# Variance over rows on one core: the first load issued as eight strided loads, ahead of the critical section

## The chip, the cores and the metric

The kernel runs on one core of a Trainium2 chip. The metric is device time in microseconds, the median of several executions. An execution under the hardware profiler gives the trace that is read here: times in it count from the first instruction of the profiled execution, and its span ends with the last one.

## The reference

```python
batch, seq, dim = 32, 512, 1024
x = np.random.randn(batch, seq, dim).astype(np.float32)
mean_sq = np.mean(x**2, axis=-1)
sq_mean = np.mean(x, axis=-1)**2
return (mean_sq - sq_mean).astype(np.float32)
```

There are 16,384 rows of 1,024 float32 values, 67.1 MB. Each row gives one number, its variance. Every byte of x is read once, and the output is 64 KB.

## The kernel before

**Layout.** The 16,384 rows are spread over 128 partitions as 128 columns, so that a "column" is one row of x on each partition. `BLOCKS` (L42) maps columns to rows: columns 0 to 15 are the first 2,048 rows, with 16 consecutive rows (64 KB) on each partition; the other 112 columns follow in the same way, with 112 consecutive rows on each partition.

**Loads.** All loads and stores are issued by SyncE (SP), in program order. Columns 0 to 95 come in six loads of 16 columns (8.4 MB each, 64 KB per partition) into two buffers in turn, `xt[0]` and `xt[1]` (L146 to L149). The first two loads wait for nothing. Each later one waits until VectorE has counted up `done` for the group that used the buffer before (L148). The last 32 columns (the end) come in loads of 8, 8, 5, 4, 2, 2, 1 and 1 columns and two halves of one column, each with a semaphore of its own (L151 to L160). The loads' helper is `load` (L89), and its DMA instruction stands on L93. A load raises its semaphore by 16 when it has landed.

**Compute.** Of each group of 16 columns, ScalarE takes 6 (`NACT`) and VectorE 10. ScalarE makes a mean in one pass (L117) and the sum of squared deviations in a second (L122). VectorE takes statistics of the two halves of a column (L113) and joins them (L216). VectorE waits for `landed` in a loop of 3 turns (L203 to L217), tells ScalarE by `go`, and after the group counts `done`. The waits in the loops are made by `take` (L107), which waits and then subtracts; its instructions stand on L109. GpSimd copies the results of a turn (L165) and joins a part of the end columns.

**The end.** The columns of the end are split over ScalarE and VectorE by `END_WHO`. Three stores (L100) follow one another: columns 0 to 15, then to the end of the fourth end load, then the rest. SP issues the last store when ScalarE and VectorE have done their last columns (L302, L303).

**Order and sections.** Tiles and semaphores come from the tile framework's pools. The whole work stands in one critical section (L144), which the framework opens with a signal from GpSimd and closes with a drain on every engine that reports to GpSimd. Behind it the context is closed (L306 to L308): two all-engine barriers, between which GpSimd clears the framework's semaphores. Only then SP waits for the three stores (L309) and clears their semaphore (L310). In the profile, the start-up of the program (constants and an all-engine barrier) stands on L325, the section's own instructions on L144, the closing on L308.

Of the kernel before, what the change touches and what calls it, by code (L numbers as in the profile page):

```python
# [11 lines left out]
def kernel(  # L12
# [14 lines left out]
    nc = tc.nc  # L27
# [9 lines left out]
    ncols = N // P  # L37
# [18 lines left out]
    EARLY = 4  # L56
    HEAD = 128

    pool = ctx.enter_context(tc.tile_pool(name="pool", bufs=1))
    xt = [pool.tile([P, GROUP, D], FP32, name=f"xt{b}") for b in range(NBUF)]  # L60
    xt_end = pool.tile([P, ncols - END0 - FIRST, D], FP32, name="xt_end")
    mv = pool.tile([P, 2, ncols], FP32, name="mv")
    stage = pool.tile([P, PER_TURN, 2], FP32, name="stage")
    stats = pool.tile([P, PER_TURN, 2, 6], FP32, name="stats")
    stats_join = pool.tile([P, JOINED, 2, 6], FP32, name="stats_join")
    stats_end = pool.tile([P, ncols - END0, 4, 6], FP32, name="stats_end")
    neg_mean = pool.tile([P, PER_TURN], FP32, name="neg_mean")
    neg_mean_end = pool.tile([P, ncols - END0], FP32, name="neg_mean_end")
    two = pool.tile([P, JOINED, 2], FP32, name="two")
    mu = pool.tile([P, JOINED, 1], FP32, name="mu")  # L70
    dev = pool.tile([P, JOINED, 4], FP32, name="dev")
    psum = ctx.enter_context(tc.tile_pool(name="psum", bufs=1, space=bass.MemoryType.PSUM))
    junk = [pool.tile([P, D], mybir.dt.bfloat16, name=f"junk{i}") for i in range(ACT_BATCH)]
    junk_sq = [psum.tile([P, D], FP32, name=f"junk_sq{i}") for i in range(ACT_BATCH)]

    sync, act, dve, gps = nc.sync, nc.scalar, nc.vector, nc.gpsimd
    landed = [tc.alloc_semaphore(f"landed{b}") for b in range(NBUF)]
    NEND = len(END_LOADS) + len(PIECES)
    landed_end = [tc.alloc_semaphore(f"landed_end{b}") for b in range(NEND)]
    go = tc.alloc_semaphore("go")  # L80
    act_done = tc.alloc_semaphore("act_done")
    done = tc.alloc_semaphore("done")
    copied = tc.alloc_semaphore("copied")
    dve_step = tc.alloc_semaphore("dve_step")
    act_step = tc.alloc_semaphore("act_step")
    gps_step = tc.alloc_semaphore("gps_step")
    stored = nc.alloc_semaphore("stored")

    def load(dst, c0, n, sem, f0=0, f=D):  # L89
        b0, pitch, row0 = next(b for b in BLOCKS if b[0] <= c0 < b[0] + b[1])  # L90
        assert c0 + n <= b0 + pitch
        ap = [[pitch * D, P], [D, n], [1, f]] if n > 1 else [[pitch * D, P], [1, f]]
        sync.dma_start(  # L93
            out=dst,
            in_=dataclasses.replace(xf, offset=(row0 + c0 - b0) * D + f0, ap=ap),
        ).then_inc(sem, 16)
# [47 lines left out]
    with tc.tile_critical(sync_engine=ENG.Pool, no_gpsimd_drain=True):  # L144

        for g in range(TURNS * NBUF):  # L146
            if g >= NBUF:
                sync.wait_ge(done, g - NBUF + 1)  # L148
            load(xt[g % NBUF], g * GROUP, GROUP, landed[g % NBUF])  # L149
        sync.wait_ge(done, (TURNS - 1) * NBUF + 1)  # L150
        c = END0  # L151
        for b, n in enumerate(END_LOADS):
            k = c - END0
            buf, k = (xt[0], k) if k < FIRST else (xt_end, k - FIRST)
            load(buf[:, k : k + n, :] if n > 1 else buf[:, k, :], c, n, landed_end[b])
            c += n
        f = 0
        for b, n in enumerate(PIECES, len(END_LOADS)):
            load(end_col(c)[:, f : f + n], c, 1, landed_end[b], f, n)
            f += n  # L160

        gps.sem_inc(copied, 1)
        for t in range(TURNS):
            gps.wait_ge(done, (t + 1) * NBUF)
            gps.tensor_copy(  # L165
                out=mv[:, 1, t * PER_TURN : (t + 1) * PER_TURN], in_=stage[:, :, 1]
            ).then_inc(copied, 1)

        part = stats_join.rearrange("p n h (e s) -> p n (h e) s", s=3)
        mean, m2 = part[:, :, :, 1], part[:, :, :, 2]  # L170
        gps.wait_ge(dve_step, 1)
        steps = [
            lambda: gps.tensor_tensor(out=two, in0=mean[:, :, 0:2], in1=mean[:, :, 2:4], op=ALU.add),  # L173
            lambda: gps.tensor_tensor(out=mu, in0=two[:, :, 0:1], in1=two[:, :, 1:2], op=ALU.add),
            lambda: gps.tensor_scalar(out=mu, in0=mu, scalar1=0.25, scalar2=None, op0=ALU.mult),
            lambda: gps.tensor_tensor(out=dev, in0=mean, in1=mu.to_broadcast([P, JOINED, 4]), op=ALU.subtract),
            lambda: gps.tensor_tensor(out=dev, in0=dev, in1=dev, op=ALU.mult),
            lambda: gps.tensor_scalar(out=dev, in0=dev, scalar1=D / 4.0, scalar2=None, op0=ALU.mult),  # L178
            lambda: gps.tensor_tensor(out=dev, in0=dev, in1=m2, op=ALU.add),
            lambda: gps.tensor_tensor(out=two, in0=dev[:, :, 0:2], in1=dev[:, :, 2:4], op=ALU.add),  # L180
            lambda: gps.tensor_tensor(out=mu, in0=two[:, :, 0:1], in1=two[:, :, 1:2], op=ALU.add),
        ]
        k = 0
        runs = []
        for j, c in enumerate(joined):
            if runs and runs[-1][1] + runs[-1][2] == c:
                runs[-1][2] += 1
            else:
                runs.append([j, c, 1])
        for j, c, n in runs:  # L190
            steps.append(
                lambda j=j, c=c, n=n: gps.tensor_scalar(  # L192
                    out=mv[:, 1, c : c + n], in0=mu[:, j : j + n, 0],
                    scalar1=1.0 / D, scalar2=None, op0=ALU.mult,
                )
            )
        for k, step in enumerate(steps):
            if k:
                gps.wait_ge(gps_step, k)
            step().then_inc(gps_step, 1)  # L200
        gps_steps = len(steps)

        with nc.Fori(0, TURNS, engines=[ENG.DVE]):  # L203
            take(dve, copied, 1)
            for b in range(NBUF):
                take(dve, landed[b], 16)
                dve.sem_inc(go, 1)
                mine = range(b * GROUP + NACT, (b + 1) * GROUP)
                for j in mine:
                    last = halves(stats[:, j, :, :], xt[b][:, j - b * GROUP, :])  # L210
                last.then_inc(dve_step, 1)
                take(dve, dve_step, 1)
                for j in mine:
                    if j == mine[-1]:
                        take(dve, act_done, 1)
                    last = dve.bn_aggr(out=stage[:, j, :], in_=stats[:, j, :, :])  # L216
                last.then_inc(done, 1)  # L217
        n = 0
        waiting = None
        seen = -1  # L220
        for b, c, who in end_cols:
            if who != "D":
                continue
            if b != seen:
                dve.wait_ge(landed_end[b], 16)
                seen = b
            col = end_col(c)
            if c in joined:
                last = halves(stats_join[:, joined.index(c), :, :], col)
                if c == joined[-1]:  # L230
                    last.then_inc(dve_step, 1)
                    n += 1
                continue
            st = stats_end[:, c - END0, :2, :]
            dve.bn_stats(out=st[:, 0, :], in_=col[:, :H])  # L235
            if waiting:
                waiting()
            n += 1
            dve.bn_stats(out=st[:, 1, :], in_=col[:, H:]).then_inc(dve_step, 1)  # L239
            dve_step_of.setdefault(b, n)  # L240

            def waiting(n=n, c=c, st=st):
                dve.wait_ge(dve_step, n)
                return dve.bn_aggr(out=mv[:, :, c], in_=st)  # L244

        c = ncols - 1
        st = stats_end[:, c - END0, : len(PIECES), :]
        f = 0
        for i, size in enumerate(PIECES):
            dve.wait_ge(landed_end[len(END_LOADS) + i], 16)  # L250
            last = dve.bn_stats(out=st[:, i, :], in_=end_col(c)[:, f : f + size])  # L251
            if i == 0:
                waiting()
            f += size
        n += 1
        last.then_inc(dve_step, 1)
        dve.wait_ge(dve_step, n)
        dve.bn_aggr(out=mv[:, :, c], in_=st).then_inc(dve_step, 1)
        dve_steps = n + 1

        act.preload_act_table(ACTF.Square)  # L261
# [15 lines left out]
        for b in range(len(END_LOADS)):  # L277
            mine = [c for bb, c, who in end_cols if bb == b and who == "A"]
            if not mine:
                continue  # L280
# [60 lines left out]
```

## Time and profile before

| What | Value |
|---|---|
| Median of 3 executions | 163.78 us (163.43 to 163.83) |
| The profiled execution's own time | 163.64 us |
| Its span, first to last instruction | 161.9 us |
| VectorE busy | 103.7 us (64%) |
| ScalarE busy | 106.3 us (66%) |
| DMA packets of SP's queue, share of 16 engines | 96.7% |
| Mean rate over the span | 415 GB/s |
| First VectorE statistics start | 23.11 us |
| Second group's statistics start | 42.44 us |
| Last store issued | 160.06 us |

The profiled execution's time is 1.7 us longer than its span, and lies 0.14 us below the median. The DMA share is the mean over the core's 16 DMA engines of the time that their packets take. Packets of the six large loads are 64 KB each, one for each partition, so that each of the 16 engines carries 8 packets of a load.

### The profile page before, as it was taken

To read this page: it belongs to the slowest core of one execution; us is meant where nothing else is said; L and a number is where in the kernel's file an instruction comes from. 1 tells how busy PE (TensorE), PEld (TensorE's weight loads), DVE (VectorE), ACT (ScalarE), POOL (GpSimd) and SP (SyncE) were. 2 spreads that over 40 slices of the span, in tenths; PEclk is the share of its full clock that TensorE was granted. 3 is DMA by queue.
4 is the path that set the end of the run, shared out by engine and by line. 5 is a ranking of instruction groups with operands and counts; after the bars stand their busy time and mean duration, and the time that the engine had idled before them with its cause. 6 is when DMAs were issued, how large, how long until landed. Compare 5 with 4: busy or idle time off the path is not lost. (4 is left out here: it accounts for less than half of the span.)

```text
span 161.9 us, 579 instructions
## 1 busy us (share of the span) xinstructions
DVE 103.7 (64%) x232; ACT 106.3 (66%) x189; POOL 3.6 (2%) x18
## 2 busy tenths in 40 slices
DVE  0000029980599607994099921999039979999994
ACT  3000029990599807996099941999139999799985
POOL 0000000000000000000000000000000000005100
DMA  7969979989988998998997997997989999999991
GB/s 263 518 275 502 518 324 453 518 356 421 518 389 389 518 405 372 518 421 356 518 437 340 518 437 340 518 470 308 518 348 429 421 470 405 400 434 411 423 394 27
DMA packets 2738, 67.19 MB, mean 415 GB/s; under 512 B 688, under 2 KB 688, under 8 KB 1200
## 3 DMA queue, kind: packets, MB, share of 16 engines
q1 hardware_dynamic: 2736, 67.18, 96.7%
q14 instruction: 2, 0.02, 0.1%
HBM read 67.11 MB, written 0.07 MB: 415 GB/s over the span
## 5 line engine op out<-in xcount | busy, mean ns | idle before, releaser
L113 DVE BATCH_NORM_STATS2 stats<-xt 128x6 f32<-128x512 f32 x120 | 71.8, 678 | 49.9 <-DVEq L109 49.9
L117 ACT ACTIVATE junk<-xt 128x1024 bf16<-128x1024 f32 x41 | 42.7, 1042 | 50.4 <-ACTq L109 49.3
L122 ACT ACTIVATE junk_sq<-xt,neg_mean 128x1024 f32<-128x1024 f32 x36 | 39.7, 1104 | 1.5
L113 DVE BATCH_NORM_STATS2 stats_join<-xt 128x6 f32<-128x512 f32 x22 | 13.2, 677 | 0.0
L216 DVE BATCH_NORM_AGGREGATE stage<-stats 128x2 f32<-128x12 f32 x60 | 6.0, 166 | 6.2 <-DVEq L109 5.3
L117 ACT ACTIVATION_READ_ACCUMULATOR junk<-xt 128x1 f32 x41 | 7.6, 186 | 0.0
L122 ACT ACTIVATE junk_sq<-xt_end,neg_mean_end 128x1024 f32<-128x1024 f32 x6 | 6.7, 1111 | 0.1
L122 ACT ACTIVATION_READ_ACCUMULATOR junk_sq<-xt,neg_mean 128x1 f32 x36 | 6.7, 186 | 0.0
L117 ACT ACTIVATE junk<-xt_end 128x1024 bf16<-128x1024 f32 x6 | 6.3, 1046 | 0.4 <-DMA xt_end<-in_x_dram 0.2
L235 DVE BATCH_NORM_STATS2 stats_end<-xt_end 128x6 f32<-128x512 f32 x9 | 6.1, 675 | 0.0
L239 DVE BATCH_NORM_STATS2 stats_end<-xt_end 128x6 f32<-128x512 f32 x9 | 5.8, 642 | 0.0
L122 ACT ACTIVATE junk_sq<-xt,neg_mean_end 128x1024 f32<-128x1024 f32 x5 | 5.5, 1106 | 0.1
L165 POOL COPY mv<-stage 128x32 f32<-128x32 f32 x3 | 0.6, 210 | 133.0 <-DVE stage L216 133.0
L261 ACT ACT_TABLE_LOAD x1 | 1.3, 1283 | 1.3 <-PEq L325 1.3
L244 DVE BATCH_NORM_AGGREGATE mv<-stats_end 128x2 f32<-128x12 f32 x9 | 1.7, 191 | 0.0
L251 DVE BATCH_NORM_STATS2 stats_end<-xt_end 128x6 f32<-128x512 f32 x2 | 1.3, 668 | 0.1
L117 ACT ACTIVATION_READ_ACCUMULATOR junk<-xt_end 128x1 f32 x6 | 1.1, 188 | 0.0
L122 ACT ACTIVATION_READ_ACCUMULATOR junk_sq<-xt_end,neg_mean_end 128x1 f32 x6 | 1.1, 186 | 0.0
L122 ACT ACTIVATION_READ_ACCUMULATOR junk_sq<-xt,neg_mean_end 128x1 f32 x5 | 0.9, 188 | 0.0
L173 POOL TENSOR_TENSOR two<-stats_join 128x22 f32<-128x22 f32 x1 | 0.3, 252 | 12.9 <-DVE stats_join L113 12.9
L192 POOL TENSOR_SCALAR mv<-mu 128x6 f32<-128x6 f32 (+1 forms) x2 | 0.5, 236 | 0.2
L178 POOL TENSOR_SCALAR dev<-dev 128x44 f32<-128x44 f32 x1 | 0.3, 331 | 0.1
(12 smaller groups left out, 2.3 us busy)
## 6 DMA issues: line engine op xcount, KB each, us to landing
xt<-in_x_dram SPq DMA_DIRECT2D x2, 4096.0 KB, 19.5
xt_end<-in_x_dram SPq DMA_DIRECT2D x1, 2560.0 KB, 29.8
xt_end<-in_x_dram SPq DMA_DIRECT2D x1, 2048.0 KB, 34.2
xt_end<-in_x_dram SPq DMA_DIRECT2D x2, 1024.0 KB, 37.1
xt_end<-in_x_dram SPq DMA_DIRECT2D x2, 512.0 KB, 39.3
xt_end<-in_x_dram SPq DMA_DIRECT2D x2, 256.0 KB, 40.0
xt<-in_x_dram SPq DMA_DIRECT2D x6, 24.5
out_dram<-mv SPq DMA_DIRECT2D x1, 52.5 KB, 4.4
```

The lines of the kernel that those rows point to most:

```text
L113: last = dve.bn_stats(out=st[:, h, :], in_=xcol[:, h * H : (h + 1) * H])
L117: return act.activation(out=junk[i], in_=xcol, func=ACTF.Copy, scale=-S / D, accum_out=nm)
L122: return act.activation(out=junk_sq[i], in_=xcol, func=ACTF.Square, scale=S, bias=nm, accum_out=var)
L165: gps.tensor_copy(out=mv[:, 1, t * PER_TURN : (t + 1) * PER_TURN], in_=stage[:, :, 1]).then_inc(copied, 1)
L173: lambda: gps.tensor_tensor(out=two, in0=mean[:, :, 0:2], in1=mean[:, :, 2:4], op=ALU.add),
L192: lambda j=j, c=c, n=n: gps.tensor_scalar(out=mv[:, 1, c : c + n], in0=mu[:, j : j + n, 0], scalar1=1.0 / D, scalar2=None, op0=ALU.mult,)
L216: last = dve.bn_aggr(out=stage[:, j, :], in_=stats[:, j, :, :])
L235: dve.bn_stats(out=st[:, 0, :], in_=col[:, :H])
L239: dve.bn_stats(out=st[:, 1, :], in_=col[:, H:]).then_inc(dve_step, 1)
L244: return dve.bn_aggr(out=mv[:, :, c], in_=st)
L251: last = dve.bn_stats(out=st[:, i, :], in_=end_col(c)[:, f : f + size])
L261: act.preload_act_table(ACTF.Square)
```

## The change

It does three things. First, the load of group 0 becomes eight DMAs. DMA p0 carries partitions p0, p0+8, p0+16, ..., p0+120, that is 16 partitions, with all 16 columns (64 KB on each). All eight raise one new semaphore, `first`; SP waits until it is 128 and then raises `landed[0]` by 16. Second, these eight DMAs and the load of group 1 are issued ahead of any critical section, and the framework's context is closed and compiled directly behind them, so that its barriers and clearing come there. Third, the rest of the program stands behind the closed context: tiles are allocated directly and not from pools, the semaphores are the kernel's own, and SP clears them, after the last store is issued and before it waits for the stores. The code of the rest is the same, one level less indented.

```diff
+    STRIDE = 8
...
-    pool = ctx.enter_context(tc.tile_pool(name="pool", bufs=1))
-    xt = [pool.tile([P, GROUP, D], FP32, name=f"xt{b}") for b in range(NBUF)]
+    def sbuf(name, shape, dtype):
+        return nc.alloc_sbuf_tensor(name, shape, dtype).ap()
+    xt = [sbuf(f"xt{b}", [P, GROUP, D], FP32) for b in range(NBUF)]
...
-    landed = [tc.alloc_semaphore(f"landed{b}") for b in range(NBUF)]
+    landed = [nc.alloc_semaphore(f"landed{b}") for b in range(NBUF)]
...
+    first = nc.alloc_semaphore("first")
     stored = nc.alloc_semaphore("stored")
+    sems = [*landed, *landed_end, go, act_done, done, copied, dve_step, act_step, gps_step, first]
...
-    with tc.tile_critical(sync_engine=ENG.Pool, no_gpsimd_drain=True):
-
-        for g in range(TURNS * NBUF):
-            if g >= NBUF:
-                sync.wait_ge(done, g - NBUF + 1)
-            load(xt[g % NBUF], g * GROUP, GROUP, landed[g % NBUF])
...
+    for p0 in range(STRIDE):
+        dma = sync.dma_start(
+            out=xt[0][p0::STRIDE, :, :],
+            in_=dataclasses.replace(
+                xf, offset=p0 * SMALL * D, ap=[[STRIDE * SMALL * D, P // STRIDE], [D, GROUP], [1, D]]
+            ),
+        ).then_inc(first, 16)
+        tc.no_tile_sem_insts.add(dma.ins.name)
+    for g in range(1, NBUF):
+        dma = load(xt[g], g * GROUP, GROUP, landed[g])
+        tc.no_tile_sem_insts.add(dma.ins.name)
     ctx.close()
     tc.close()
     tc.compile()
+
+    sync.wait_ge(first, STRIDE * 16)
+    sync.sem_inc(landed[0], 16)
+
+    for g in range(NBUF, TURNS * NBUF):
+        sync.wait_ge(done, g - NBUF + 1)
+        load(xt[g % NBUF], g * GROUP, GROUP, landed[g % NBUF])
...
     store(early, ncols)
+    sync.sem_clear(range(sems[0].num, sems[-1].num + 1))
     sync.wait_ge(stored, 48)
     sync.sem_clear(stored)
```

More of the change, by code (lines that the diff above doesn't have):

```diff
@@ L56 @@
     EARLY = 4
+    STRIDE = 8
     HEAD = 128
-    pool = ctx.enter_context(tc.tile_pool(name="pool", bufs=1))
-    xt = [pool.tile([P, GROUP, D], FP32, name=f"xt{b}") for b in range(NBUF)]
[L61 to L73, printed above, removed]
@@ L74, with psum @@
-    junk_sq = [psum.tile([P, D], FP32, name=f"junk_sq{i}") for i in range(ACT_BATCH)]
+    def sbuf(name, shape, dtype):
+        return nc.alloc_sbuf_tensor(name, shape, dtype).ap()
+    def psum(name, shape, dtype):
+        return nc.alloc_psum_tensor(name, shape, dtype).ap()
+    xt = [sbuf(f"xt{b}", [P, GROUP, D], FP32) for b in range(NBUF)]
+    xt_end = sbuf("xt_end", [P, ncols - END0 - FIRST, D], FP32)
+    mv = sbuf("mv", [P, 2, ncols], FP32)
+    stage = sbuf("stage", [P, PER_TURN, 2], FP32)
@@ new lines @@
+    stats = sbuf("stats", [P, PER_TURN, 2, 6], FP32)
+    stats_join = sbuf("stats_join", [P, JOINED, 2, 6], FP32)
+    stats_end = sbuf("stats_end", [P, ncols - END0, 4, 6], FP32)
+    neg_mean = sbuf("neg_mean", [P, PER_TURN], FP32)
+    neg_mean_end = sbuf("neg_mean_end", [P, ncols - END0], FP32)
+    two = sbuf("two", [P, JOINED, 2], FP32)
+    mu = sbuf("mu", [P, JOINED, 1], FP32)
+    dev = sbuf("dev", [P, JOINED, 4], FP32)
+    junk = [sbuf(f"junk{i}", [P, D], mybir.dt.bfloat16) for i in range(ACT_BATCH)]
@@ L76 @@
+    junk_sq = [psum(f"junk_sq{i}", [P, D], FP32) for i in range(ACT_BATCH)]
     sync, act, dve, gps = nc.sync, nc.scalar, nc.vector, nc.gpsimd
-    landed = [tc.alloc_semaphore(f"landed{b}") for b in range(NBUF)]
+    landed = [nc.alloc_semaphore(f"landed{b}") for b in range(NBUF)]
     NEND = len(END_LOADS) + len(PIECES)
[L79 to L86, printed above, removed]
+    landed_end = [nc.alloc_semaphore(f"landed_end{b}") for b in range(NEND)]
+    go = nc.alloc_semaphore("go")
+    act_done = nc.alloc_semaphore("act_done")
+    done = nc.alloc_semaphore("done")
+    copied = nc.alloc_semaphore("copied")
+    dve_step = nc.alloc_semaphore("dve_step")
+    act_step = nc.alloc_semaphore("act_step")
@@ L87 @@
+    gps_step = nc.alloc_semaphore("gps_step")
+    first = nc.alloc_semaphore("first")
     stored = nc.alloc_semaphore("stored")
+    sems = [*landed, *landed_end, go, act_done, done, copied, dve_step, act_step, gps_step, first]
     def load(dst, c0, n, sem, f0=0, f=D):
@@ L92, in load @@
         ap = [[pitch * D, P], [D, n], [1, f]] if n > 1 else [[pitch * D, P], [1, f]]
-        sync.dma_start(
+        return sync.dma_start(
             out=dst,
@@ L142 @@
         engine.addr_align(FETCH_BLOCK_INSTRUCTIONS, offset=HEAD, max_nops=0)
-    with tc.tile_critical(sync_engine=ENG.Pool, no_gpsimd_drain=True):
-        for g in range(TURNS * NBUF):
-            if g >= NBUF:
-                sync.wait_ge(done, g - NBUF + 1)
-            load(xt[g % NBUF], g * GROUP, GROUP, landed[g % NBUF])
[L150 to L261, printed above, removed]
-        with nc.Fori(0, TURNS, engines=[ENG.Activation]):
-            for b in range(NBUF):
-                take(act, go, 1)
-                for i0 in range(0, NACT, ACT_BATCH):
-                    mine = range(b * GROUP + i0, b * GROUP + i0 + ACT_BATCH)
-                    for i, j in enumerate(mine):
-                        last = act_mean(i, xt[b][:, i0 + i, :], neg_mean[:, j : j + 1])
-                    last.then_inc(act_step, 1)
-                    take(act, act_step, 1)
-                    for i, j in enumerate(mine):
-                        last = act_var(
-                            i, xt[b][:, i0 + i, :], neg_mean[:, j : j + 1], stage[:, j, 1:2]
-                        )
-                last.then_inc(act_done, 1)
-        n = 0
[L277 to L280, printed above, removed]
-            act.wait_ge(landed_end[b], 16)
-            for i, c in enumerate(mine):
-                k = c - END0
-                last = act_mean(i, end_col(c), neg_mean_end[:, k : k + 1])
-            n += 1
-            last.then_inc(act_step, 1)
-            act.wait_ge(act_step, n)
-            for i, c in enumerate(mine):
-                k = c - END0
-                last = act_var(i, end_col(c), neg_mean_end[:, k : k + 1], mv[:, 1, c : c + 1])
-            n += 1
-            last.then_inc(act_step, 1)
-            act_step_of[b] = n
-        act_steps = n
-        sync.wait_ge(copied, 1)
-        store(0, SMALL)
-        sync.wait_ge(gps_step, gps_steps)
-        sync.wait_ge(act_step, act_step_of[EARLY - 1])
-        sync.wait_ge(dve_step, dve_step_of[EARLY])
-        store(SMALL, early)
-        sync.wait_ge(act_step, act_steps)
-        sync.wait_ge(dve_step, dve_steps)
-        store(early, ncols)
@@ L308 @@
     tc.compile()
+    sync.wait_ge(first, STRIDE * 16)
[3 more added lines that the diff above has]
+        load(xt[g % NBUF], g * GROUP, GROUP, landed[g % NBUF])
+    sync.wait_ge(done, (TURNS - 1) * NBUF + 1)
+    c = END0
+    for b, n in enumerate(END_LOADS):
+        k = c - END0
+        buf, k = (xt[0], k) if k < FIRST else (xt_end, k - FIRST)
+        load(buf[:, k : k + n, :] if n > 1 else buf[:, k, :], c, n, landed_end[b])
+        c += n
@@ new lines @@
+    f = 0
+    for b, n in enumerate(PIECES, len(END_LOADS)):
+        load(end_col(c)[:, f : f + n], c, 1, landed_end[b], f, n)
+        f += n
+    gps.sem_inc(copied, 1)
+    for t in range(TURNS):
+        gps.wait_ge(done, (t + 1) * NBUF)
+        gps.tensor_copy(
+            out=mv[:, 1, t * PER_TURN : (t + 1) * PER_TURN], in_=stage[:, :, 1]
+        ).then_inc(copied, 1)
+    part = stats_join.rearrange("p n h (e s) -> p n (h e) s", s=3)
+    mean, m2 = part[:, :, :, 1], part[:, :, :, 2]
@@ new lines @@
+    gps.wait_ge(dve_step, 1)
+    steps = [
+        lambda: gps.tensor_tensor(out=two, in0=mean[:, :, 0:2], in1=mean[:, :, 2:4], op=ALU.add),
+        lambda: gps.tensor_tensor(out=mu, in0=two[:, :, 0:1], in1=two[:, :, 1:2], op=ALU.add),
+        lambda: gps.tensor_scalar(out=mu, in0=mu, scalar1=0.25, scalar2=None, op0=ALU.mult),
+        lambda: gps.tensor_tensor(out=dev, in0=mean, in1=mu.to_broadcast([P, JOINED, 4]), op=ALU.subtract),
+        lambda: gps.tensor_tensor(out=dev, in0=dev, in1=dev, op=ALU.mult),
+        lambda: gps.tensor_scalar(out=dev, in0=dev, scalar1=D / 4.0, scalar2=None, op0=ALU.mult),
+        lambda: gps.tensor_tensor(out=dev, in0=dev, in1=m2, op=ALU.add),
+        lambda: gps.tensor_tensor(out=two, in0=dev[:, :, 0:2], in1=dev[:, :, 2:4], op=ALU.add),
+        lambda: gps.tensor_tensor(out=mu, in0=two[:, :, 0:1], in1=two[:, :, 1:2], op=ALU.add),
+    ]
@@ new lines @@
+    k = 0
+    runs = []
+    for j, c in enumerate(joined):
+        if runs and runs[-1][1] + runs[-1][2] == c:
+            runs[-1][2] += 1
+        else:
+            runs.append([j, c, 1])
+    for j, c, n in runs:
+        steps.append(
+            lambda j=j, c=c, n=n: gps.tensor_scalar(
+                out=mv[:, 1, c : c + n], in0=mu[:, j : j + n, 0],
+                scalar1=1.0 / D, scalar2=None, op0=ALU.mult,
+            )
+        )
+    for k, step in enumerate(steps):
+        if k:
+            gps.wait_ge(gps_step, k)
+        step().then_inc(gps_step, 1)
@@ new lines @@
+    gps_steps = len(steps)
+    with nc.Fori(0, TURNS, engines=[ENG.DVE]):
+        take(dve, copied, 1)
+        for b in range(NBUF):
+            take(dve, landed[b], 16)
+            dve.sem_inc(go, 1)
+            mine = range(b * GROUP + NACT, (b + 1) * GROUP)
+            for j in mine:
+                last = halves(stats[:, j, :, :], xt[b][:, j - b * GROUP, :])
+            last.then_inc(dve_step, 1)
+            take(dve, dve_step, 1)
+            for j in mine:
+                if j == mine[-1]:
+                    take(dve, act_done, 1)
+                last = dve.bn_aggr(out=stage[:, j, :], in_=stats[:, j, :, :])
+            last.then_inc(done, 1)
@@ new lines, with waiting @@
+    n = 0
+    waiting = None
+    seen = -1
+    for b, c, who in end_cols:
+        if who != "D":
+            continue
+        if b != seen:
+            dve.wait_ge(landed_end[b], 16)
+            seen = b
+        col = end_col(c)
+        if c in joined:
+            last = halves(stats_join[:, joined.index(c), :, :], col)
+            if c == joined[-1]:
+                last.then_inc(dve_step, 1)
+                n += 1
+            continue
+        st = stats_end[:, c - END0, :2, :]
+        dve.bn_stats(out=st[:, 0, :], in_=col[:, :H])
+        if waiting:
+            waiting()
+        n += 1
+        dve.bn_stats(out=st[:, 1, :], in_=col[:, H:]).then_inc(dve_step, 1)
+        dve_step_of.setdefault(b, n)
+        def waiting(n=n, c=c, st=st):
+            dve.wait_ge(dve_step, n)
+            return dve.bn_aggr(out=mv[:, :, c], in_=st)
@@ new lines @@
+    c = ncols - 1
+    st = stats_end[:, c - END0, : len(PIECES), :]
+    f = 0
+    for i, size in enumerate(PIECES):
+        dve.wait_ge(landed_end[len(END_LOADS) + i], 16)
+        last = dve.bn_stats(out=st[:, i, :], in_=end_col(c)[:, f : f + size])
+        if i == 0:
+            waiting()
+        f += size
+    n += 1
+    last.then_inc(dve_step, 1)
+    dve.wait_ge(dve_step, n)
+    dve.bn_aggr(out=mv[:, :, c], in_=st).then_inc(dve_step, 1)
+    dve_steps = n + 1
+    act.preload_act_table(ACTF.Square)
@@ new lines @@
+    with nc.Fori(0, TURNS, engines=[ENG.Activation]):
+        for b in range(NBUF):
+            take(act, go, 1)
+            for i0 in range(0, NACT, ACT_BATCH):
+                mine = range(b * GROUP + i0, b * GROUP + i0 + ACT_BATCH)
+                for i, j in enumerate(mine):
+                    last = act_mean(i, xt[b][:, i0 + i, :], neg_mean[:, j : j + 1])
+                last.then_inc(act_step, 1)
+                take(act, act_step, 1)
+                for i, j in enumerate(mine):
+                    last = act_var(
+                        i, xt[b][:, i0 + i, :], neg_mean[:, j : j + 1], stage[:, j, 1:2]
+                    )
+            last.then_inc(act_done, 1)
@@ new lines @@
+    n = 0
+    for b in range(len(END_LOADS)):
+        mine = [c for bb, c, who in end_cols if bb == b and who == "A"]
+        if not mine:
+            continue
+        act.wait_ge(landed_end[b], 16)
+        for i, c in enumerate(mine):
+            k = c - END0
+            last = act_mean(i, end_col(c), neg_mean_end[:, k : k + 1])
+        n += 1
+        last.then_inc(act_step, 1)
+        act.wait_ge(act_step, n)
+        for i, c in enumerate(mine):
+            k = c - END0
+            last = act_var(i, end_col(c), neg_mean_end[:, k : k + 1], mv[:, 1, c : c + 1])
+        n += 1
+        last.then_inc(act_step, 1)
+        act_step_of[b] = n
@@ L309 @@
+    act_steps = n
+    sync.wait_ge(copied, 1)
+    store(0, SMALL)
+    sync.wait_ge(gps_step, gps_steps)
+    sync.wait_ge(act_step, act_step_of[EARLY - 1])
+    sync.wait_ge(dve_step, dve_step_of[EARLY])
+    store(SMALL, early)
+    sync.wait_ge(act_step, act_steps)
+    sync.wait_ge(dve_step, dve_steps)
+    store(early, ncols)
+    sync.sem_clear(range(sems[0].num, sems[-1].num + 1))
     sync.wait_ge(stored, 48)
```

## The prediction, made before the change was run

> **What bounds the kernel now.** I read the page first, then the busy time by stages, then the waits, then the chain that ended last, and at the end the instructions of the closing line. The page's DMA part says that the transfers hardly ever rest:
>
> ```profile
> q1 hardware_dynamic: 2736, 67.18, 96.7%
> ...
> HBM read 67.11 MB, written 0.07 MB: 415 GB/s over the span
> ```
>
> The stages, cut at about one 8.4 MB load each (length, VectorE, ScalarE and GpSimd busy, clock, DMA share, GB/s), say where the missing 3.3% lies:
>
> ```profile
> 1.50:5.50 4.00, 0.00 (x0) 1.08 (x1) 0.00 (x0) 1.00 1.30 512
> ...
> 24.00:43.30 19.30, 12.94 (x31) 13.33 (x25) 0.00 (x0) 1.00 1.00 435
> 43.30:62.70 19.40, 13.01 (x31) 13.40 (x25) 0.21 (x1) 1.00 1.00 432
> ```
>
> In a steady stage the share is 1.00, at 432 to 435 GB/s, while the two compute engines are busy for 13 of 19.3 us. So time is lost only before the first packet and after the last. The waits agree: per group, both engines stand still until data land.
>
> ```profile
> SPq L93 <- DVE stage L216: 111.4, 5, 35.4
> ...
> DVE stats L113 <- DVEq L109: 49.9, 6, 23.1
> ACT junk L117 <- ACTq L109: 49.3, 6, 20.6
> ```
>
> The first line counts for nothing: SP waits for a free buffer, but group 2 is issued at 37.1 us and group 1 lands at 42.2, so 5 us of transfers are still queued. The chain ends thus (start, length, what):
>
> ```profile
> 117.84 39.74 DMA xt_end<-in_x_dram
> 157.58 0.02 issue
> 157.61 1.16 ACT junk L117 x2
> 158.76 0.02 issue
> 158.79 1.12 ACT junk_sq L122
> ```
>
> It is transfers up to 157.58, then one column on ScalarE. VectorE is nearly as late (last join from 159.68 for 0.21 us). Both anchor to landings, so whatever shifts the transfers as a whole shifts the end by the same amount.
>
> **The trace's packet records**, which my sums use: the first 64 KB packets start between 1.89 and 3.21 us and take 2.42 to 3.17 us (median 2.86). After that each takes 2.418 us, whichever load it belongs to: 65,536 B in 2.418 us is 27.1 GB/s per engine, times 16 is 434. Eight packets are 19.34 us, and load after load lands 19.3 us after the one before (22.89, 42.21, 61.56, ...). The last engine of load 0 lands 0.75 us after the first one (22.14 to 22.89), and this lag persists to the end of the kernel (0.71 us in the last load).
>
> **Part 1: first DMA earlier.** SP's start barrier is through at 0.655 us. Then come a branch of the section at 0.716 and the first DMA at 0.869. Issued outside a section it can stand where the branch does: -0.15 us. Bounds: 0 to -0.21.
>
> **Part 2: closing the context in front.** What goes is at the end:
>
> ```profile
> L308 SPq EVENT_SEMAPHORE  x4: 17/17/27, 160.6 to 161.8; - x4
> ...
> L308 POOLq EVENT_SEMAPHORE_RANGE_CLEAR  x2: 64/101/138, 161.1 to 161.4; - x2
> ```
>
> The last store is issued at 160.06 and lands at 161.46 (1.4 us). SP leaves the closing barriers at 161.81 and clears at 161.87 for 0.025, which ends the span. Without barriers the landing is late next: 161.46, some 0.04 for the wait, 0.025 for the clear, 161.53. So -0.36 us. The added clear of the semaphores on SP (GpSimd's took 0.064 to 0.138) lies beside the store's 1.4 us, and the section's drains (SP's took 0.13) go too, under the same cover. In front, the same barriers and clears (about 1.1 us here, 160.7 to 161.8) now run on each engine behind SP's nine DMA issues. An issue takes 0.43 us with none waiting (0.869 to 1.302), so SP comes to them at 0.72 + 9 x 0.43 = 4.6 us and is through by 6. Nobody needs an engine before the first landing at 22: 16 us of cover. Were the closing to wait for the loads, the cover would be gone: VectorE would start near 42 instead of 23, and group 2 would be issued 14 us after the queue had run dry. Nothing in the diff makes a drain wait for a DMA, so I give that under 1 in 100.
>
> **Part 3: the hand-over of group 0.** SP waits for 128, then adds 16: two instructions of about 0.02 us, plus a signal. It delays the first VectorE work by about 0.1 us. Group 0 then has done at 37.2 rather than 37.1, against 5 us of queued transfers: 0. Behind SP's wait stand only the later loads, which need that same done.
>
> **Part 4: eight DMAs of 16 partitions.** The bytes are the same, and each engine still carries eight packets of 64 KB if a DMA is shared out one partition per engine. Seven DMAs are added, 7 x 0.43 = 3.0 us of issue on SP, but the second is issued 0.43 us after the first, while each engine is busy for 2.4 us with its packet: hidden. Load 1 is queued at about 4.2 us instead of 1.3, long before 20: hidden. Seven more completions per engine: the regular interval of 19.3 us, against 8 x 2.418, leaves no room for a price of one: 0.
>
> *Gain.* Only 16 packets have to be handed out before all engines run, not 128. If this is what spread the starts over 1.32 us, the lagging engine gains at most that. If the lag comes from the two instruction fetches recorded at 1.77 and 1.92 us, it gains nothing. I take -0.5 us, two thirds of the lasting lag of 0.75; bounds 0 to -1.3.
>
> *Loss.* Before, the sixteen packets in flight go to whichever partitions the single DMA gives the engines; now they always go to partitions 8 apart. The trace never shows this set together. A single partition takes 27.1 GB/s, since one packet is one partition; what two neighbours on a common path would take, no row says. The near row for two streams on one path is an 8 KB instruction packet among the x packets: 0.50 and 0.86 us, where alone it took 0.31, so 1.6 to 2.8 times, about a halved rate. If the paths into the partitions are as wide as the engines (27.1) and the sixteen partitions meet two by two, each packet takes 2 x 2.418, and load 0 38.7 us: +19.3. If they don't meet, or the paths have room, 0. An in-between price is the start itself: if each of the eight pays the first packets' excess (2.86 - 2.42), +3.5.
>
> [...]
>
> From the rows alone I also lean to the loss: no packet in the steady loads ever beats 2.418 us, no laggard makes up its lag, and one rate holds for row pitches of 64 KB and of 448 KB, so the limit is not the source's. It sits in the engine or at the destination, and when the ends are this far apart the nearest row is the shared one. Against it: the instruction fetches, with another destination, run at 8,192 B in 0.307 us, 26.7 GB/s, so the engine alone explains the rate.
>
> Nothing in the 137 us behind load 0 can take back such a loss: the stages there are at share 1.00.
>
> **The sum**, against the profiled execution's 163.64: -0.15 - 0.36 + 0 - 0.5 = -1.0, and +19.3: 181.9. That execution lies 0.14 below the median, so 182.1 as a median. The gains' bounds (-0.36 to -1.9), and the meeting engines not being in step by the 1.3 us that their starts were apart (which spares that much), give this case 179.8 to 183.3.
>
> **Rivals.**
> 1. *No shared path.* The gains alone: 163.78 - 1.0 = 162.8, bounds 161.9 to 163.4. For it: the engine-bound reading above; one partition per engine at a time is what the kernel does already.
> 2. *Start price eight times.* 163.78 - 1.0 + 3.5 = 166.3. Against it: the excess appears only in the first packets, and later loads start without any.
> 3. *Nothing measurable.* The gains at their small end, 163.4, within 0.3% (0.49 us, about what a measurement of this kernel can tell from no change). The other code layout may also cost VectorE or ScalarE an instruction fetch in the last columns, where VectorE is busy without a gap from 133.8 on; a packet of 0.3 to 0.86 us would take back the gain.
>
> **How the numbers follow.** Shared path 0.58, start price or other small losses 0.03, nothing measurable 0.04, no shared path 0.35. The first decides the predicted time, 182.1, with its own range 179.8 to 183.3. Leaving out either large case leaves out more than 2 in 10, so the range takes in both: 162.2 to 183.3. Faster 0.35, same 0.04, slower 0.61.
>
> **What would show it.** Shared path: load 0's packets take about 4.84 us after the first, VectorE starts at about 41 us instead of 23.1, the first 40 us run at about 217 GB/s, later stages stay at 432 to 435. No shared path: packets of 2.418 us, VectorE at 21.8 to 22.9. In both: the closing barriers between 1 and 6 us, and the end about 0.07 us after the last store has landed. I am wrong if load 0's packets are unchanged, or if something other than load 0 loses time.

## The result and the profile after

The changed kernel takes 184.7 us (184.61 to 184.79), the one before 163.7 us: a ratio of 1.128, 95% interval 1.127 to 1.129. The sign that was forecast came true, and so did the mechanism, packets that get in each other's way at the partitions they are written to (5.11 us each and not 2.42; 5.10 with the same partitions and another source, in e3); the time lies 1.4 us above the range. "Path" is the prediction's word for a way into the partitions that several of them have in common; the traces show no paths, only how long the packets to a set of partitions take. Times in the traces are each those of one execution.

The page of the changed kernel, first its slices (40 of 4.6 us: share of the DMA engines' time in tenths, then GB/s), then the queue:

```profile
DMA  9999894999899999999879999999889999999992
GB/s 232 229 229 229 172 200 100 214 229 386 357 400 458 458 458 458 458 458 443 386 329 443 458 458 458 458 458 458 386 357 400 458 450 422 401 429 417 411 399 61
...
q1 hardware_dynamic: 2848, 67.18, 97.1%
...
HBM read 67.11 MB, written 0.07 MB: 366 GB/s over the span
```

The share of engine time is as high as before (97.1% against 96.7%), and the rate is halved in the first nine slices. That is the lesson of these two rows: the share says that packets are under way, not that they are fast. Stages of the same kernel (columns as in the prediction; a packet counts in the stage in which it starts):

```profile
5.50:24.00 18.50, 0.00 (x0) 1.28 (x1) 0.00 (x0) 1.00 1.10 227
24.00:43.30 19.30, 0.00 (x0) 0.00 (x0) 0.00 (x0) 1.00 0.93 211
44.50:63.90 19.40, 13.19 (x31) 13.58 (x25) 0.00 (x0) 1.00 1.00 432
```

Behind group 0 everything runs at 432 GB/s again. The waits show who paid: the longest wait of VectorE was 23.1 us and is 44.5 now.

```profile
DVE stats L120 <- DVEq L116: 71.1, 6, 44.5
ACT junk L124 <- ACTq L116: 64.6, 6, 36.0
```

In the packet records, the eight packets that each DMA engine carries for group 0 take 4.87, 5.11, 5.11, 5.11, 4.88, 5.11, 5.11 and 5.11 us (medians over the 16 engines); later ones take 2.42 us as before. Group 0 lands at 44.20 us, not 22.89: +21.31. The last store is issued at 181.90 and not 160.06: +21.84. The span ends 1.44 us behind that, not 1.84: -0.40. The sum is 21.44, the difference of the spans (183.34 and 161.89). The times of the two profiled executions differ by only 21.02 (184.66 and 163.64): 1.75 us lay outside the span before, and 1.32 now.

The other half microsecond (21.84 against 21.31) comes late. The end of the chain of waits, then the waits of the last columns, and under them the only such line of the kernel before:

```profile
138.92 40.51 DMA xt_end<-in_x_dram
179.43 0.02 issue
179.45 1.16 ACT junk L124 x2
```

```profile
ACT junk L124 <- DMA xt_end<-in_x_dram: 1.0, 2, 0.8
DVE stats_end L273 <- DMA xt_end<-in_x_dram: 0.7, 1, 0.7
```

```profile
ACT junk L117 <- DMA xt_end<-in_x_dram: 0.2, 1, 0.2
```

Before, the last ScalarE column landed 1.27 us after the load in front of it (156.31 to 157.58); now it is 1.94 (177.49 to 179.43). At 176.83 an 8 KB instruction fetch is recorded on the DMA engines, among the last small loads. Of the 16 engines' landings of the load that came in at 179.43, fifteen lie between 178.20 and 178.78, and one 0.64 us behind them. In the kernel before, the first fetch after those at 1.77 and 1.92 came at 162.18, behind the end of the span.

### The profile page after: what moved, and what is told of

Same layout as the page of the kernel before. It is cut to its first block, busy times and chain, and to the rows that moved or that the text cites. A ratio compares the mean times of both kernels' runs of the same rounds, so it can differ in the third digit from the quotient of the medians.

```text
span 183.3 us, 569 instructions
## 1 busy us (share of the span) xinstructions
DVE 103.7 (57%) x232; ACT 106.3 (58%) x189; POOL 3.6 (2%) x18
## 3 DMA queue, kind: packets, MB, share of 16 engines
q1 hardware_dynamic: 2848, 67.18, 97.1%
```

## The experiments

Two questions stood: what makes group 0's packets slow, and what the new order of the program costs without them. Where a kernel is called "the new order", it is the changed kernel with group 0 in one DMA.

### One load in the new order (e1)

```diff
-    for p0 in range(STRIDE):
-        dma = sync.dma_start(out=xt[0][p0::STRIDE, :, :], ...).then_inc(first, 16)
+    dma = load(xt[0], 0, GROUP, landed[0])
...
-    sync.wait_ge(first, STRIDE * 16)
-    sync.sem_inc(landed[0], 16)
```

> The changed kernel with group 0 loaded by one DMA on all 128 partitions again; the loads ahead of the section, the closed context in front and the own semaphores stay. Theory (the loss is all in which 16 partitions are written together): packets of 2.418 us, group 0 lands near 22.7 us, and what is left are the gains of the first DMA 0.15 us earlier and of the end without barriers, 0.4 us: 163.2 us against 163.7, ratio 0.997. Rival (the new order of sections costs time too): 163.7 or more. Open beside it: whether the instruction fetch in the last loads, which held one DMA engine back by 0.66 us in the changed kernel, comes with the new layout (then 163.2 becomes 163.8).

Measured: 164.32 us, ratio 1.0046 (1.0032 to 1.0060). The packets are at 2.42 us again, group 0 lands at 23.10, so the theory of the packets holds. But the new order was to gain half a microsecond and loses 0.8 (164.32 against 163.56): a miss for the main number, in the direction that the text left open. A fetch stands at 155.9 us; the landings of one load are spread over 1.1 us up to then (before: 0.7, so group 0 lands at 23.10 and not at the expected 22.7) and 2.07 behind it (155.44 to 157.51).

### Eight blocks of 16 neighbours (e2)

```diff
-            out=xt[0][p0::STRIDE, :, :],
+            out=xt[0][p0 * (P // STRIDE) : (p0 + 1) * (P // STRIDE), :, :],
...
-                xf, offset=p0 * SMALL * D, ap=[[STRIDE * SMALL * D, P // STRIDE], [D, GROUP], [1, D]]
+                xf, offset=p0 * (P // STRIDE) * SMALL * D, ap=[[SMALL * D, P // STRIDE], [D, GROUP], [1, D]]
```

> The changed kernel, but DMA p0 carries 16 neighbouring partitions (16 p0 to 16 p0 + 15) in place of every eighth; source rows are then 64 KB apart from engine to engine, not 512 KB. [...] Rival A (a source pitch of 512 KB is slow): packets of 2.418 us, 163.3 us. Rival B (DMAs of 16 partitions or eight completions are slow as such): packets of 5.1 us, 184.7 us.

Measured: 219.0 us in one run; packets of 9.38 us, group 0 lands at 78.4. The stage row (40 us into group 0):

```profile
50.00:60.00 10.00, 0.00 (x0) 0.00 (x0) 0.00 (x0) 1.00 0.94 105
```

Sixteen packets start in these 10 us, hence the 105; 16 packets in 9.38 us are 112 GB/s. Same bytes, same number of DMAs, a quarter of the steady 432 GB/s. Rivals A and B are out. A packet takes 3.9 times 2.418 us.

### The same partitions from a contiguous source (e3)

```diff
-                xf, offset=p0 * SMALL * D, ap=[[STRIDE * SMALL * D, P // STRIDE], [D, GROUP], [1, D]]
+                xf, offset=p0 * (P // STRIDE) * SMALL * D, ap=[[SMALL * D, P // STRIDE], [D, GROUP], [1, D]]
```

> The changed kernel with the same eight DMAs to every eighth partition, but DMA p0 reads 1 MB in one piece (rows 256 p0 to 256 p0 + 255), so that engines read 64 KB apart and not 512 KB apart. The results of columns 0 to 15 so belong to other rows than their places in the output say; the work is the same. Theory (the destination decides): packets of 5.11 us as before, 184.7 us. Rival (the source pitch decides): packets of 2.418 us, 163.3 us.

Measured: 184.8 us in one run, packets of 5.10 us against 5.11. The source pitch explains 0.2% of a packet; the destination decides.

### Eight loads by columns (e4)

```diff
-            out=xt[0][p0::STRIDE, :, :],
+            out=xt[0][:, 2 * p0 : 2 * p0 + 2, :],
...
-                xf, offset=p0 * SMALL * D, ap=[[STRIDE * SMALL * D, P // STRIDE], [D, GROUP], [1, D]]
+                xf, offset=2 * p0 * D, ap=[[SMALL * D, P], [D, 2], [1, D]]
```

> The changed kernel with group 0 in eight DMAs of all 128 partitions and two columns each (packets of 8 KB in place of 64 KB). Theory (number of DMAs costs nothing, the set of partitions does): 8 KB packets of 0.31 us, so 64 of them 19.8 to 20.0 us an engine, group 0 lands near 23.3 us, 163.7 us or 0.3 to 0.6 more than the kernel with one load. Rival (eight DMAs or the hand-over cost the time): near 184 us. It also asks whether smaller first packets let the engines start closer together: then up to 0.5 us less.

Measured: 164.61 us, ratio 1.0061 (1.0047 to 1.0075), 0.29 above e1; packets of 0.309 us; group 0 lands at 23.87. Eight DMAs with their hand-over are not what costs 21 us. The engines don't come closer together either: the landings of each of the eight DMAs are spread over 1.34 to 1.36 us. The late fetch is there too (156.6).

### Every second partition (e5)

```diff
-    STRIDE = 8
+    STRIDE = 2
```

> The changed kernel with group 0 in two DMAs of every second partition (64 partitions each), so four packets per engine and DMA. [...] Reading B (what counts is how many paths the partitions of a DMA reach in all; every second partition reaches all of them): packets of 2.418 us, 164 us.

Measured: 163.7 us in one run, packets of 2.418 us, group 0 lands at 22.96. That is what reading B forecast: 64 partitions at the packet time of all 128. The records show neither paths nor which engine carried which partition. A late fetch is here too (155.7).

### The strided loads in the old order (e7)

```diff
+    first = tc.alloc_semaphore("first")
...
+            if g == 0:
+                for p0 in range(8):
+                    sync.dma_start(out=xt[0][p0::8, :, :], ...).then_inc(first, 16)
+                continue
+            if g == NBUF:
+                sync.wait_ge(first, 128)
+                sync.sem_inc(landed[0], 16)
```

> The kernel before with the eight strided DMAs and their hand-over alone: the section, the pools and the closing at the end stay. Theory (the whole loss is the shared paths, +21.3 us with the start): group 0's packets 5.11 us, no fetch in the last loads: 163.6 + 21.6 = 185.1 us, ratio 1.131. Rival (a part of the 21 us is the new order's): 184 us or less.

Measured: 184.94 us, ratio 1.130 (1.128 to 1.132). Group 0 lands at 44.02, packets of 5.10, no late fetch. The strided loads alone make +21.3 us. The rest of the change is worth -0.2 us on top of them (184.70 against 184.94) and +0.8 us without them (e1): it is small beside the 21 us.

### Strided loads for group 1 (e8)

```diff
+    dma = load(xt[0], 0, GROUP, landed[0])
...
-            out=xt[0][p0::STRIDE, :, :],
+            out=xt[1][p0::STRIDE, :, :],
...
-    for g in range(1, NBUF):
-        dma = load(xt[g], g * GROUP, GROUP, landed[g])
...
-    sync.wait_ge(first, STRIDE * 16)
-    sync.sem_inc(landed[0], 16)
...
+    gps.wait_ge(first, STRIDE * 16)
+    gps.sem_inc(landed[1], 16)
```

> The new order with one load for group 0, and group 1 in eight DMAs of every eighth partition instead; GpSimd hands it over. Theory (shared paths, anywhere in the stream): group 0 lands at 23.1 us, group 1's packets take 5.11 us and it lands 40.6 us after group 0 and not 19.3, 164.3 + 21.4 = 185.7 us if the late fetch is there, 184.9 if not. Rival (a price of the start): group 1 lands 19.3 to 23 us after group 0, 164 to 168 us.

Measured: 186.2 us in one run. Group 0 lands at 24.40 and group 1 at 64.93, 40.5 us later. It is no price of the start. A late fetch is here too (178.1).

### Halves (e6)

```diff
-    STRIDE = 8
+    STRIDE = 2
...
-            out=xt[0][p0::STRIDE, :, :],
+            out=xt[0][p0 * (P // STRIDE) : (p0 + 1) * (P // STRIDE), :, :],
```

> The changed kernel with group 0 in two DMAs, of partitions 0 to 63 and of 64 to 127. [...] Reading C (all 16 engines carry it, two to a path): packets of 5.1 us, group 0 lands at 43 to 44 us, 184.7 us. [...]

Measured: 184.9 us in one run, packets of 5.12 us on all 16 engines. That is reading C. The stages from 20 to 30 us, first of the halves, then of every second partition:

```profile
20.00:30.00 10.00, 0.00 (x0) 0.00 (x0) 0.00 (x0) 1.00 1.01 210
```

```profile
20.00:30.00 10.00, 6.78 (x12) 6.62 (x12) 0.00 (x0) 1.00 1.01 439
```

Both kernels use two DMAs of 64 partitions; which 64 differs, and with them the source's pitch, 64 KB for the halves and 128 KB for every second one (at 64 KB the kernel before reads at the full rate). One stands at 210 GB/s, the other at 439. These rows count whole packets that start in 10 us; from the packets' own times it is 16 in 5.12 us, 205 GB/s, and 16 in 2.418 us, 434.

### The alignment behind the closing (e9), for VectorE alone (e10)

By its arguments, `addr_align` puts the code that follows on an engine at slot `HEAD` of a block of instructions. In the new order the closing's instructions come between it and the loops.

```diff
-    for engine in (act, dve):
-        engine.addr_align(FETCH_BLOCK_INSTRUCTIONS, offset=HEAD, max_nops=0)
...
     tc.compile()
+    for engine in (act, dve):
+        engine.addr_align(FETCH_BLOCK_INSTRUCTIONS, offset=HEAD, max_nops=0)
```

> The kernel with one load for group 0 in the new order, with the alignment of ScalarE's and VectorE's code moved from ahead of the closed context to behind it. Theory (the new order costs 0.8 us because one of these two engines, with the closing's instructions between the alignment and its code, now fetches 8 KB of instructions among the last loads, which holds one DMA engine back): no fetch between 100 us and the last landing, the last load's landings spread by 0.7 to 1.1 us and not 2.0, time 163.2 to 163.5 against 164.3 with the fetch and 163.6 before. Rival (the fetch is SyncE's or GpSimd's, or the end is late for another reason): fetch at 155.9 us again, 164.3.

Measured: 163.55 us, ratio 0.9987 (0.9977 to 0.9997). The late fetch is gone, the last load's landings are spread over 1.2 us and not 2.0. The time is just above what was expected. Two fetches come at 7.4 us instead, into the running loads, and group 0's landings are spread over 1.22 us; that this is the reason isn't shown, since the span is no longer than the one before (161.89 us both).

> As the one before, but with VectorE's alignment alone moved behind the closed context, ScalarE's left ahead of it. If the late fetch is VectorE's (it starts 0.05 us after one of its instructions in two kernels), it goes: 163.2 to 163.5. If it is ScalarE's (0.6 us after one of its instructions), it stays at 155.9: 164.3.

Measured (the same move for `dve` alone, `act` stays in front): 163.3 us in one run, no late fetch. So the late fetch hangs on where VectorE's code lies.

### A smaller offset in front (e11)

```diff
-    HEAD = 128
+    HEAD = 96
```

> The kernel with one load for group 0 in the new order, with both alignments ahead of the closed context as in the changed kernel, but 32 slots earlier in the fetch block (offset 96, not 128). Theory (VectorE's code runs over the end of its fetch block among the last loads): the late fetch goes, no fetch is added at 7.4 us as there was with the alignment behind, 163.1 to 163.4 us against 163.6 before. Rival (the block is not what decides): fetch at 155.9 us, 164.3.

Measured, on the new order and for both engines: 163.14 us, ratio 0.9966 (0.9954 to 0.9977). This is the fastest kernel here, and the new order without its late fetch. Of the 0.56 us between its profiled execution and that of the kernel before, 0.13 lies in the span and 0.43 outside it. The ends of the chains, first of e1, then of e11:

```profile
118.08 40.69 DMA xt_end<-in_x_dram
158.78 0.02 issue
158.80 1.16 ACT junk L124 x2
```

```profile
118.08 39.77 DMA xt_end<-in_x_dram
157.85 0.02 issue
157.87 1.16 ACT junk L124 x2
```

The same loads, issued at the same time, land 0.92 us earlier. Two fetches remain, at 38.6 and 38.8 us; the spread of the landings grows from 0.54 (group 0) to 1.10 (group 2) across them, and it stays at 1.10 up to the last small loads. So an early fetch can leave a lag too, and the theory that a place without fetches had been found is only half true.

### The same fetch in the kernel before (e12)

```diff
-    for engine in (act, dve):
-        engine.addr_align(FETCH_BLOCK_INSTRUCTIONS, offset=HEAD, max_nops=0)
+    for engine, head in ((act, HEAD), (dve, 152)):
+        engine.addr_align(FETCH_BLOCK_INSTRUCTIONS, offset=head, max_nops=0)
```

> The kernel before, with VectorE's alignment alone moved 24 slots later in its fetch block (offset 152, not 128), nothing else. Theory (a fetch of 8 KB among the last small loads holds one DMA engine back for good): a fetch of about 0.33 us between 145 and 158 us, landings of the last loads spread over 1.3 to 2 us and not 0.7, 164.1 to 164.7 us, ratio 1.003 to 1.007. Rival (the late landings of the new order have another cause): 163.6, ratio 1.000, with or without a fetch.

Measured: 164.38 us, ratio 1.0043 (1.0028 to 1.0058). The fetch came earlier than expected, at 142.98 us (0.325 long). The landings are spread over 0.63 us up to the load in front of it and over 1.35 behind it (144.59 to 145.94), and this stays to the end. The waits of e12's last columns; the kernel before has the first line the same, the second with 0.2 us, and neither of the others:

```profile
ACT junk L117 <- DMA xt<-in_x_dram: 1.1, 1, 1.1
ACT junk L117 <- DMA xt_end<-in_x_dram: 0.7, 2, 0.4
DVE stats_end L251 <- DMA xt_end<-in_x_dram: 0.5, 1, 0.5
DVE stats_end L235 <- DMA xt_end<-in_x_dram: 0.2, 1, 0.2
```

Both directions are shown: moving VectorE's code alone takes a late fetch away in the new order and brings one into the old, for 1.0 us (164.32 against e10's single 163.27) and 0.7 us (164.38 against 163.66).

## Why the prediction was right, and where it was wrong

**What bounds the kernel: right.** Transfers set the end; of the 21.3 us lost in group 0 the stages behind it took 0.13 us back, and then the last column came 0.67 us later.

**Part 4, the loss: the mechanism is right, its size is the step that failed.** The term was "each packet takes 2 x 2.418, and load 0 38.7 us: +19.3". A packet of group 0 takes 5.112 us, 0.276 more than twice 2.418. That sixteen partitions 8 apart meet two by two on a path, and that sharing is free of loss, were assumptions; no run shows them. What the runs showed in their place is that the partitions written together decide: packets of 5.11 us for every eighth partition, 5.12 for halves, 2.418 for every second one and 9.38 for blocks of 16. Two packets of group 0 together move 131,072 B in 5.112 us, 25.6 GB/s, where one packet of 2.418 us moves at 27.1. From the last engine's start to the last packet's end pass 40.1 us (3.36 to 43.47) and not 38.7, and the load then lands 0.73 us behind that end, where the single DMA took 0.35 (22.54 to 22.89). The sum had no term for this second delay.

**Part 4, the gain: wrong.** "I take -0.5 us" had its lower bound, 0, come true: the last engine of group 0 lands 0.75 us after the first one (43.44 to 44.20), as before. The first packets start from 2.08 to 3.36 us, before from 1.89 to 3.21. An issue on SP takes 0.59 us where the single DMA took 0.38, eight of them follow one another 0.64 us apart and not 0.43, and the first packet comes 1.36 us after the first issue began (before: 1.02), which ate the 0.15 us of part 1.

**Part 1: right in itself** (first issue at 0.715, -0.154), of no use to the changed kernel. In e11 the first packet starts 0.15 us earlier, at 1.74, and group 0 lands at 22.55.

**Part 2: right in the span.** -0.36 forecast, -0.40 measured behind the last store. The closing barriers run from 6.5 to 7.1 us, a little later than forecast because of the longer issues; only ScalarE's table load waits for them, at 7.2 us, which costs nothing. Outside the span a further 0.43 us went, for which the forecast had no term: in every kernel of the old order that was run, 1.7 to 1.8 us of the time lie outside the span, in most of the new order 1.3 to 1.4, and with the alignment behind the closing (e9, e10) 1.35 to 1.72. What happens there isn't in the traces. What I left out of the main sum is that the closing's instructions shift VectorE's code. Rival 3 named an instruction fetch in the last columns with a price of 0.3 to 0.86; one came, and the last column landed 0.67 us later, but not because VectorE was held up: one of the 16 DMA engines that all loads need was late.

**Part 3: right.** VectorE starts 0.26 us after group 0 has landed, before it was 0.22, and this costs nothing.

**The balance.** The forecast's terms up to the landing of group 0 were +19.34 - 0.15 - 0.5 = +18.69 us; measured are +21.31, 2.6 more: 1.4 from the packets (40.1 against 38.7), 0.4 from the landing behind them, 0.5 for the gain that didn't come, 0.3 for starts that came 0.15 us later and not earlier. The end of the kernel adds 0.5 (the late fetch), and the time outside the span takes 0.4. With the forecast's 18.3 us (182.1 against 163.78) this makes 21.0, and 21.0 are measured. The range had room for less loss (engines out of step), for none above 2 x 2.418, and for no extra landing time, which is why 184.7 fell outside. By its own terms its upper end is even lower than stated: 163.78 + 19.34 - 0.36 is 182.8, and no term stands for the rest up to 183.3.

**The weighing of the rows.** The argument that the fetches' 26.7 GB/s leave the engine as the only limit was the wrong reading: in every one of these kernels 16 packets of 64 KB are under way at a time, and they take 2.418 us for all partitions and for every second one, 5.112 and 5.12 for every eighth and for halves, and 9.376 for blocks of 16 (434, 205 and 112 GB/s). The set of partitions sets a limit of its own, below that of the engines. The number of DMAs doesn't: two DMAs of every second partition (e5) ran at the full rate, two of halves (e6) at half of it, and eight by columns (e4) cost 0.29 us over one.

What stays open: whether there are paths that packets share, as the prediction has it, and why two packets of group 0 move 25.6 GB/s in all, less than one at 2.418 us; why the load of such packets lands later behind its last packet (0.73 us and not 0.35); why one packet of group 0 after the first is shorter, the fifth, in the changed kernel (4.88 us), in e7 (4.90) and with halves (4.95), where the second half begins; which engine carries which partition; and why a fetch of 0.33 us makes a lag of 0.6 to 1.0 us. In e2 each DMA goes to other partitions than the one before and the engines are 1.4 us apart, so packets of two DMAs may run side by side for a part of the time; 9.376 us need not be what 16 neighbours alone would take.

## What to carry to other kernels

Before a load is split by partitions, measure the packets for the partitions of each piece: pieces by columns (0.309 us for 8 KB) and every second partition (2.418 us for 64 KB) kept the rate here, halves (5.12) and every eighth partition (5.11) halved it, and blocks of 16 neighbours (9.38) left about a quarter. The share of busy DMA time did not show this loss (97.1% against 96.7%); the GB/s of the stage did (227 and 211 against 432). Moving set-up code about can also bring a late instruction fetch among the loads: moving VectorE's alignment alone took one away in e10 (163.27 us against e1's 164.32) and brought one in e12 (164.38 against 163.66). In a kernel bound by transfers, look for instruction packets among the loads, the early ones too (e11: 38.6 and 38.8 us), and try a shift of the code if there is one.

## What the runs showed of the hardware that was not expected

- One engine moves 27.1 GB/s (65,536 B in 2.418 us) in the steady loads. With every eighth partition a packet takes 5.112 us, and two of them together move 25.6: less than one of the steady packets. With blocks of 16 partitions a packet takes 9.376 us.
- In these runs an 8 KB instruction fetch among the running loads left one DMA engine late for the rest of the kernel: landings spread wider by 0.67 us in the changed kernel, 0.95 in e1, about 0.7 in e12, for packets of 0.33 us. Among loads at the full rate no run shows an engine making up its lag (0.74 us in group 0 and 0.72 in the last but one load of the kernel before). Where group 0 was slow the lag shrank: in e2 from 1.41 us in group 0 to 0.42 in group 1, in the changed kernel from 1.04 to 0.57.
- Two DMAs of 64 partitions each, once every second partition and once 64 neighbours, differ by a factor of 2.1 (packets of 2.418 and 5.12 us, 434 and 205 GB/s).
